# Rope's cosine product on VectorE from PSUM, its sum and a subtraction on GpSimd

## The chip, the cores and the metric

The kernel runs on one core of a Trainium2 chip. A core has five engines with a queue each: TensorE (PE in the profile; its weight loads are PEld), VectorE (DVE), ScalarE (ACT), GpSimd (POOL) and SyncE (SP), which here only issues transfers. Each engine works through its queue in order; an instruction that waits holds up everything behind it on that engine. The metric is the device time of one execution in microseconds, the median of several.

## The reference

One decoder layer on 512 tokens of width 1024, in float32, with two token mixers side by side and an MLP:

```python
h = rms_norm(x, norm_mix)
u, q, kc, vc, ksl, vsl, kwn, vwn, g_nsa, g_merge = split(h @ w_in)
y_pool = pool_mixer(u, ...)                    # causal means over 2, 4, 8, 16 tokens
y_nsa  = nsa_mixer(q, kc, vc, ksl, vsl, kwn, vwn, g_nsa, ...)
merged = sigmoid(g_a) * (y_pool @ w_proj_pool) + sigmoid(g_b) * (y_nsa @ w_proj_nsa)
x = x + merged @ w_out
x = x + square(relu(rms_norm(x, norm_mlp) @ w_ff1)) @ w_ff2
return rms_norm(x, norm_final)
```

The attention mixer has 16 heads of 64 in two groups. Each head has three branches: compressed keys (31 per group), selected blocks, and a window; with 512 tokens the last two are plain causal attention on keys of their own. Queries and keys are rotated first:

```python
def apply_rope(x, cos, sin):
    x1, x2 = split(x, 2, axis=-1)
    rot = concatenate([-x2, x1], axis=-1)
    return x * cos + rot * sin
```

Each softmax subtracts a row's extreme before the exponential. For the compressed branch that is a separate step, and the change touches it.

## The kernel before, in words

Matrix products run in a split form: each float32 operand becomes a high part and a low part (ScalarE copies the high part, VectorE or GpSimd subtracts it from the original for the low part), and three of the four partial products are summed. The weights are loaded in pieces of 512 KB by SyncE and split shortly before use (L345 and L347).

**Stages.** Up to about 30 us the input is normed and transposed. Up to about 175 us the projections run (function `fm`, matmuls at L388), among them the two key projections and the first three query pairs, each followed by a rope. Then comes attention, to about 395 us, and after it the output projections and the MLP.

**Attention.** Work is cut into 96 slots, twelve for each of eight pairs of heads. For slot i the loop at L1096 issues the scores of slot i+1 on TensorE (L977), the transposes of slot i-4's probabilities (L1039, into `psT`) and their evacuation (L1050 on ScalarE, L1054 on VectorE), the masking and row minimum of slot i on VectorE (L999), its exponential on ScalarE (L1009), and the weighting of slot i-1's probabilities on GpSimd (L1022, which needs the reciprocal of L1019 on VectorE). The product with the values (L1073) follows two slots after the transposes. In between, TensorE runs pieces of the remaining projections (the filler: five query pairs and the merge gate).

**Side work.** Generators in the list `side` advance by one step, to their next `yield`, once in each slot (`step_side`, L1121). Two kinds matter here. `rope` (L575) turns one projection of 128 rows and 512 tokens: ScalarE copies it from PSUM to `xr` with a scale, four transfers copy 32-row blocks of `xr` crosswise into `sw`, then come two products with the cosine table in halves of 256 columns (L589, in place in `xr`), two with the sine table (L592, in `sw`), and two sums (L597). Products run on GpSimd when `mode["pool"]` is set, which it is from attention on (five ropes), and on VectorE before (five ropes); the sums run on VectorE always. Then `done` splits the result into high and low part: for queries ScalarE copies at L622 and L623, and VectorE subtracts at L625 and L627. `cmp_scores` (L909) makes the compressed branch's probabilities of one pair: matmuls (L914), mask (L921, L922) and row minimum (L924) on VectorE, the subtraction of the minimum (L926), the exponential on ScalarE (L929), sum and reciprocal on VectorE (L931 to L934), scaling and split on GpSimd (L936 to L939), then transposes (L947) and a copy on ScalarE (L949). There are eight of these.

**What sets the order.** The code above gives program order. The framework's planner then orders each engine's queue: among the instructions that it takes to be ready it prefers the one that is earliest in the program. Operations that the program issues in different slots can so stand next to each other in a queue. `tc.issue_after` pins an instruction behind another one; GpSimd also issues transfers (L267) that add pairs of weight blocks for the MLP, in some slots behind the weighting.

Of the kernel before, what the change touches and what calls it, by code (L numbers as in the profile page):

```python
# [13 lines left out]
F32 = mybir.dt.float32  # L14
FR = mybir.dt.float32r
AF = mybir.ActivationFunctionType
ALU = mybir.AluOpType
# [3 lines left out]
S = 512  # L21
# [41 lines left out]
def trunk(ctx: ExitStack, tc: tile.TileContext, A, out):  # L63
    nc = tc.nc
    PE, ACT, DVE, POOL = nc.tensor, nc.scalar, nc.vector, nc.gpsimd
    PSUM = bass.MemoryType.PSUM

    def pool(name, **kw):
        return tc.tile_pool(name=name, bufs=1, reuse_waits="tile", **kw)
# [400 lines left out]
    op = e2.enter_context(pool("op"))  # L470
# [3 lines left out]
    ap = at.enter_context(pool("att"))  # L474
# [91 lines left out]
    cosT, sinT = cst[:, C_COS:C_COS + S], cst[:, C_SIN:C_SIN + S]  # L566
# [8 lines left out]
    def rope(ps, scale, done, after=0):  # L575

        assert not scored["rope"]
        scored["rope"] = 1
        xr = ap.tile([128, S], F32, tag="rx", bufs=1, name="rx")
        sw = ap.tile([128, S], F32, tag="rs", bufs=1, name="rs")  # L580
        ACT.activation(xr, ps, AF.Copy, scale=scale)
        for b in range(4):
            a = b ^ 1
            nc.sync.dma_start(sw[32 * b:32 * b + 32, :], xr[32 * a:32 * a + 32, :])
        yield
        eng = POOL if mode["pool"] else DVE
        hs = [slice(0, S // 2), slice(S // 2, S)]
        for c in hs:
            eng.tensor_tensor(xr[:, c], xr[:, c], cosT[:, c], op=ALU.mult)  # L589
            yield  # L590
        for c in hs:
            eng.tensor_tensor(sw[:, c], sw[:, c], sinT[:, c], op=ALU.mult)  # L592
            yield
        yield
        for c in hs:
            yield
            DVE.tensor_tensor(xr[:, c], xr[:, c], sw[:, c], op=ALU.add)  # L597
        while scored["pairs"] < after:
            yield
        for _ in done(xr):  # L600
            yield
        scored["rope"] = 0
# [28 lines left out]
    with ExitStack() as c1:  # L631
# [170 lines left out]
        def pool_out(g):  # L802
# [5 lines left out]
                                     op1=ALU.subtract)  # L808

        first_posts += [cmp_first("k"), lambda ps: rope(ps, -0.125, k_done(0))]  # L810
        next(first)
        pr = ps1.tile([128, 36], F32, tag="F", bufs=2, name="psF")
# [4 lines left out]
        for k in P1[2:]:  # L817
            i = int(k[-1]) if k[-1].isdigit() else None
            if k == "kw":
                run(fm(k, ps1, lambda ps: rope(ps, -0.125, k_done(1))))  # L820
            elif k == "cv":
                run(fm(k, ps1, cmp_first("v")))
            elif k[0] == "w" and k != "wpool":
                run(cmp_mlp1(k[1], i))
            elif k[0] == "u":
                run(fm(k, ps1, pool_mix(i)))
            elif k[0] == "q":
                run(fm(k, ps1, lambda ps, i=i: rope(ps, 1.0, q_done(i))))
            elif k == "V0":
                run(project_v())  # L830
            elif k == "wpool":
                use(k)
            elif k[:2] == "ga":
                def post(ps, j=i):
                    ACT.activation(MA[:, j, :], ps, AF.Sigmoid)  # L835
                run(fm(k, ps1, post))
                if i < 4:
                    pool_out(i)
            elif k[:2] == "pp":
                w = use(k)  # L840
                for e in range(2):
                    def post(ps, jj=2 * i + e):
                        DVE.tensor_tensor(MA[:, jj, :], ps, MA[:, jj, :], op=ALU.mult)
                    run(fm(w, ps1, post, xT=yd, sub=e, nk=4))
# [9 lines left out]
    with ExitStack() as c2:  # L854
# [54 lines left out]
        def cmp_scores(p):  # L909
            g = p // 4  # L910
            ps = ps2.tile([128, NT, 2, 64], F32, tag="S", bufs=S_BANKS, name="psC")
            for qb in range(NT):
                for h in range(2):
                    PE.matmul(ps[:, qb, h, :], Q[p][:, h, 128 * qb:128 * qb + 128], KC[g], start=True, stop=True,  # L914
                              skip_group_check=True)
            w = p2.tile([128, NT, 2, 64], F32, tag="cw", bufs=1, name="cw")
            s8 = p2.tile([128, 3, 8], F32, tag="c8", bufs=1, name="c8")
            cm = cst[:, C_CM:C_CM + 128].rearrange("p (q n) -> p q n", q=NT)
            wl = w[:, :, :, 0:32]
            wf = w.rearrange("p q h n -> p (q h) n")[:, :, 0:32]  # L920
            DVE.tensor_tensor(wl, ps[:, :, :, 0:32], cm[:, :, None, :].to_broadcast([128, NT, 2, 32]), op=ALU.add)  # L921
            DVE.tensor_tensor(wl, ps[:, :, :, 32:64], wl, op=ALU.add)  # L922
            yield
            DVE.tensor_reduce(s8[:, 0, :], wf, axis=AX.X, op=ALU.min)  # L924
            yield
            DVE.tensor_tensor(wf, wf, s8[:, 0, :, None].to_broadcast([128, 8, 32]), op=ALU.subtract)  # L926
            yield
            yield
            ACT.activation(wl, wl, AF.Exp, scale=-1.0)  # L929
            yield  # L930
            DVE.tensor_reduce(s8[:, 1, :], wf, axis=AX.X, op=ALU.add)  # L931
            DVE.reciprocal(s8[:, 2, :], s8[:, 1, :])
            r = s8[:, 2, :].rearrange("p (q h) -> p q h", q=NT)
            DVE.tensor_tensor(r, r, GT[:, :, 6 * p:6 * p + 6:3], op=ALU.mult)  # L934
            yield
            POOL.tensor_tensor(wl, wl, r[:, :, :, None].to_broadcast([128, NT, 2, 32]), op=ALU.mult)  # L936
            pH, pL = (PC[:, :, e, :].rearrange("p q (h n) -> p q h n", h=2) for e in range(2))
            POOL.tensor_scalar(pH, wl, 1.0, 1.0, op0=ALU.mult, op1=ALU.mult)
            POOL.tensor_tensor(pL, wl, pH.bitcast(F32), op=ALU.subtract)  # L939
            yield  # L940
            yield
            yield
            yield
            pt = ps2.tile([128, S], F32, tag="T", bufs=T_BANKS, name="psT")
            for qb in range(NT):
                src = PC[:, qb, :, :].rearrange("p e c -> p (e c)")
                PE.transpose(pt[:, 128 * qb:128 * qb + 128].bitcast(FR), src, identR)  # L947
            t = p2.tile([128, S], FR, tag="pc", bufs=1, name="pc")
            ACT.activation(t, pt, AF.Copy)  # L949
            PTc[p] = t  # L950
# [126 lines left out]
        def o_evac(p, half):  # L1077
# [7 lines left out]
            split_ready()  # L1085

        side.append(cmp_scores(0))
        while 0 not in PTc:
            fill()
# [6 lines left out]
        for i in range(n + LAG + PLAG):  # L1096
            if i < n:
                p = slots[i][0]
                if i % 12 == 3 and p + 1 < NPAIR:
                    while p + 1 not in Q:  # L1100
                        fill()
                        step_side()
                if i % 12 == CMP_AT and p + 1 < NPAIR:
                    side.append(cmp_scores(p + 1))
# [476 lines left out]
```

## Time and profile before

| | us |
|---|---|
| median of 3 runs (lowest to highest) | 819.68 (818.72 to 820.07) |
| profiled execution | 819.35 |
| its span, first to last instruction | 817.4 |
| TensorE busy | 791.0 (97%) |
| VectorE busy | 616.8 (75%) |
| ScalarE busy | 483.3 (59%) |
| GpSimd busy | 206.1 (25%) |

A row of the timeline has start, duration, engine, line, operation, the tiles it writes and reads, and the shapes; in brackets stands the idle time of the engine just before it and what ended it. A row of a group has the count, and the duration in ns as lowest, median and highest, or the busy sum and the mean. In a table by stretch, the busy times of PE, PEld, DVE, ACT and POOL follow the stretch's length, each with its number of instructions, then the granted TensorE clock (1.00 is full speed), the busy share of the transfer engines and their GB/s. Rows of GpSimd can overlap, since a following instruction's record begins before the one ahead has ended; the distance between starts tells what one costs in a series.

### The profile page before, as it was taken

To read this page: it belongs to the slowest core of one execution; us is meant where nothing else is said; L and a number is where in the kernel's file an instruction comes from. 1 tells how busy PE (TensorE), PEld (TensorE's weight loads), DVE (VectorE), ACT (ScalarE), POOL (GpSimd) and SP (SyncE) were. 2 spreads that over 40 slices of the span, in tenths; PEclk is the share of its full clock that TensorE was granted. 3 is DMA by queue.
4 is the path that set the end of the run, shared out by engine and by line. 5 is a ranking of instruction groups with operands and counts; after the bars stand their busy time and mean duration, and the time that the engine had idled before them with its cause. 6 is when DMAs were issued, how large, how long until landed. Compare 5 with 4: busy or idle time off the path is not lost.

```text
span 817.4 us, 13940 instructions
## 1 busy us (share of the span) xinstructions
PE 791.0 (97%) x5081; PEld 707.5 (87%) x5081; DVE 616.8 (75%) x1201; ACT 483.3 (59%) x959; POOL 206.1 (25%) x271
## 2 busy tenths in 40 slices
PE   7999999998899999999999999999999999999996
PEld 5889877886788888888787899999999999999985
DVE  7797734548979898889675479996889688987823
ACT  5566433326877888899434466844674377347711
POOL 6000000027757867765333200111010100000000
PEclk9999999999999999999999999999999999999999
DMA  9363732456537634552964716999998965345402
GB/s 304 96 176 107 203 79 92 113 155 154 78 103 136 145 83 91 104 126 56 331 159 135 206 21 186 321 241 287 252 271 228 272 185 181 123 162 180 155 1 103
DMA packets 124445, 130.85 MB, mean 160 GB/s; under 512 B 5173, under 2 KB 112217, under 8 KB 124250
## 3 DMA queue, kind: packets, MB, share of 16 engines
q1 hardware_dynamic: 105082, 110.31, 42.0%
q0 software_dynamic: 19008, 18.88, 16.2%
q8 instruction: 40, 0.66, 0.3%
q10 hardware_dynamic: 288, 0.79, 0.3%
q14 instruction: 27, 0.22, 0.1%
HBM read 125.24 MB, written 39.85 MB: 202 GB/s over the span
## 4 chain that ended last, share of the span: by engine, by line
PE 70%; DVE 16%; ACT 6%; issue 4%; DMA 2%; POOL 1%; SPq 0%; ACTq 0%; DVEq 0%; POOLq 0%
PE psF L388 21%; PE psB L1350 16%; PE psB L388 13%; PE psB L1466 7%; PE psO L1073 3%; PE psT L1039 2%; PE psS L977 2%; DVE wl L302 2%; PE psV L388 2%; DVE P L999 2%; DVE PT L1054 1%; DMA raw<-w_out 1%; ACT P L1009 1%; PE psF L442 1%; DVE w3l L302 1%
## 5 line engine op out<-in xcount | busy, mean ns | idle before, releaser
L388 PE MATMUL psF<-R,wh 128*128 128x512 f32 x512 | 166.9, 404 | 0.2 <-ACT MA L835 0.2
L300 ACT ACTIVATE wh<-raw 128x1024 fp32r<-128x1024 f32 x66 | 69.8, 1058 | 75.6 <-PE psB L1466 33.4
L345 ACT ACTIVATE wh<-raw 128x512 fp32r<-128x512 f32 (+1 forms) x102 | 61.3, 619 | 86.7 <-PE psF L388 35.8
L388 PEld LDWEIGHTS psF<-R,wh 128*128 128x128 f32 x512 | 92.5, 189 | 17.9 <-ACT MA L835 0.5
L388 PE MATMUL psF<-R,wl 128*128 128x512 f32 x256 | 101.9, 398 | 0.8 <-DVE wl L347 0.8
L1022 POOL TENSOR_SCALAR P<-P,sm,GT 128x128 f32<-128x128 f32 (+3 forms) x128 | 85.2, 698 | 47.9 <-DVE sm L1019 33.5
L302 DVE TENSOR_TENSOR wl<-raw,wh 128x1024 fp32r<-128x1024 f32 x66 | 80.7, 1222 | 17.6 <-ACT wh L300 17.5
L267 POOL DMA_DIRECT2D S<-w_ff x36 | 41.7, 1158 | 193.0 <-DMA S<-w_ff 146.3
L347 DVE TENSOR_TENSOR wl<-raw,wh 128x512 fp32r<-128x512 f32 (+1 forms) x78 | 56.2, 732 | 37.7 <-ACT wh L345 37.4
L1009 ACT ACTIVATE P<-P,sm 128x128 f32<-128x128 f32 (+3 forms) x128 | 71.1, 557 | 11.6 <-DVE sm L999 10.5
L1350 PE MATMUL psB<-R,wh 128*128 128x256 f32 x352 | 64.1, 282 | 0.0
L999 DVE CUSTOM_DVE_ANT_0 P<-psS,cst 128x128 f32<-128x128 f32 (+3 forms) x128 | 59.6, 484 | 5.9 <-PE psT L1039 4.3
L347 POOL TENSOR_TENSOR wl<-raw,wh 128x512 fp32r<-128x512 f32 x28 | 39.9, 1427 | 85.1 <-ACT wh L345 82.7
L1054 DVE TENSOR_TENSOR PT<-psT,PT 128x512 fp32r<-128x512 f32 (+2 forms) x96 | 56.7, 595 | 4.6 <-ACT PT L1050 3.6
L1050 ACT ACTIVATE PT<-psT 128x512 fp32r<-128x512 f32 (+2 forms) x96 | 49.3, 521 | 16.0 <-PE psT L1039 15.4
L388 PEld LDWEIGHTS psF<-R,wl 128*128 128x128 f32 x256 | 48.4, 189 | 11.8 <-DVE wl L347 0.9
L1039 PE MATMUL psT<-ident,P 128*128 128x128 f32 x320 | 51.3, 275 | 6.1 <-POOL P L1022 4.9
L300 ACT ACTIVATE w3h<-raw 128x1024 fp32r<-128x1024 f32 x32 | 33.8, 1057 | 38.8 <-PE psB L1466 16.5
L1039 PEld LDWEIGHTS psT<-ident,P 128*128 128x128 f32 x320 | 40.0, 141 | 17.0 <-POOL P L1022 7.8
L1350 PEld LDWEIGHTS psB<-R,wh 128*128 128x128 f32 x352 | 54.1, 189 | 0.3 <-DVE R L1292 0.2
L1350 PE MATMUL psB<-R,wl 128*128 128x256 f32 x176 | 49.5, 281 | 0.0
L302 DVE TENSOR_TENSOR w3l<-raw,w3h 128x1024 fp32r<-128x1024 f32 x32 | 39.1, 1222 | 12.9 <-ACT w3h L300 12.9
(432 smaller groups left out, 2280.3 us busy)
## 6 DMA issues: line engine op xcount, KB each, us to landing
raw<-w_ff SPq DMA_DIRECT2D x56, 512.0 KB, 4.6
S<-w_ff POOLq DMA_DIRECT2D x36, 512.0 KB, 7.6
raw<-S SPq DMA_DIRECT2D x36, 512.0 KB, 5.4
raw<-w_in SPq DMA_DIRECT2D x32, 512.0 KB, 3.9
S<-w_ff SPq DMA_DIRECT2D x28, 512.0 KB, 5.4
S<-S SPq DMA_DIRECT2D x8, 512.0 KB, 8.3
raw<-w_proj_nsa SPq DMA_DIRECT2D x8, 512.0 KB, 4.0
raw<-w_out SPq DMA_DIRECT2D x8, 512.0 KB, 4.4
```

The source lines that it names most:

```text
L300: ACT.activation(h, t, AF.Copy)
L302: DVE.tensor_tensor(l, t, h.bitcast(F32), op=ALU.subtract)
L345: ACT.activation(h[:, sl], t[:, sl], AF.Copy)
L347: eng.tensor_tensor(l[:, sl], t[:, sl], h[:, sl].bitcast(F32), op=ALU.subtract)
L388: PE.matmul(ps, a, b, start=first and j == 0, stop=last and j == n - 1, skip_group_check=True)
L999: DVE.tensor_tensor_reduce(out=P[:, o:o + n].rearrange("p (a c) -> p a c", c=128), in0=s, in1=m, scale=1.0, scalar=3e38, op0=ALU.add, op1= ...
L1009: last_exp[:] = [ACT.activation(c, c, AF.Exp, bias=sm[:, 0, e:e + 1], scale=-1.0, accum_out=sm[:, 1, e:e + 1])]
L1022: r = POOL.tensor_scalar(P[:, o:o + n], P[:, o:o + n], sm[:, 2, e:e + 1], GT[:, qb, c + e:c + e + 1], op0=ALU.mult, op1=ALU.mult)
L1039: PE.transpose(pt[:, 128 * j:128 * j + 128], P[:, 128 * j:128 * j + 128], ident)
L1054: DVE.tensor_tensor(dL, src, dH.bitcast(F32), op=ALU.subtract)
L1350: PE.matmul(out, w[u][:, k, 128 * f:128 * f + 128], XB[x][v][:, k, :], **kw)
L1466: PE.matmul(out, YB[y][u][:, k, 128 * f:128 * f + 128], w[v][:, k, :], **kw)
```

## The change

In `rope` a third tile `xc` takes the cosine product, which VectorE now makes in one instruction from PSUM with the scale in it, in the step that makes ScalarE's copy. The two steps of the old cosine products stay as empty ones, so that the sine products and the sums keep their steps. The sums go to the engine that makes the sine products, GpSimd during attention, and read `xc` in place of `xr`; they still write `xr`. In `cmp_scores` the subtraction of the minimum goes from VectorE to GpSimd.

```diff
         xr = ap.tile([128, S], F32, tag="rx", bufs=1, name="rx")
         sw = ap.tile([128, S], F32, tag="rs", bufs=1, name="rs")
+        xc = ap.tile([128, S], F32, tag="rc", bufs=1, name="rc")
         ACT.activation(xr, ps, AF.Copy, scale=scale)
         for b in range(4):
             a = b ^ 1
             nc.sync.dma_start(sw[32 * b:32 * b + 32, :], xr[32 * a:32 * a + 32, :])
+        DVE.scalar_tensor_tensor(xc, ps, scale, cosT, op0=ALU.mult, op1=ALU.mult)
         yield
         eng = POOL if mode["pool"] else DVE
         hs = [slice(0, S // 2), slice(S // 2, S)]
-        for c in hs:
-            eng.tensor_tensor(xr[:, c], xr[:, c], cosT[:, c], op=ALU.mult)
-            yield
+        yield
+        yield
         for c in hs:
             eng.tensor_tensor(sw[:, c], sw[:, c], sinT[:, c], op=ALU.mult)
             yield
         yield
         for c in hs:
             yield
-            DVE.tensor_tensor(xr[:, c], xr[:, c], sw[:, c], op=ALU.add)
+            eng.tensor_tensor(xr[:, c], xc[:, c], sw[:, c], op=ALU.add)
...
-            DVE.tensor_tensor(wf, wf, s8[:, 0, :, None].to_broadcast([128, 8, 32]), op=ALU.subtract)
+            POOL.tensor_tensor(wf, wf, s8[:, 0, :, None].to_broadcast([128, 8, 32]), op=ALU.subtract)
```

## The prediction

> **What bounds the kernel now.** I read the page first, then busy time by stretch, then TensorE's waits, and last the timelines of the two places that these point to.
>
> ```profile
> span 817.4 us, 13940 instructions
> PE 791.0 (97%) x5081; PEld 707.5 (87%) x5081; DVE 616.8 (75%) x1201; ACT 483.3 (59%) x959; POOL 206.1 (25%) x271
> ```
> ```profile
> 30.00:175.00 145.00, 144.80 (x701) 120.34 (x700) 92.75 (x182) 67.46 (x128) 2.41 (x6) 1.00 0.47 132
> 175.00:230.00 55.00, 49.01 (x280) 41.03 (x279) 44.11 (x135) 36.80 (x99) 36.75 (x53) 0.94 0.51 106
> 230.00:380.00 150.00, 147.34 (x943) 128.98 (x942) 131.40 (x435) 125.42 (x339) 104.96 (x146) 1.00 0.51 111
> 380.00:817.00 437.00, 425.63 (x3028) 397.34 (x3026) 328.69 (x421) 236.31 (x363) 48.91 (x40) 1.00 0.66 188
> ```
>
> After each stretch's length stand the busy times of PE, PEld, DVE, ACT and POOL, then the granted clock. TensorE bounds the kernel: from 30 to 175 us, where the first five ropes run, it idles 0.2 us. The stretch to look at is 175 to 230, the start of attention: 6.0 us idle (55.00 less 49.01) and a clock of 0.94. From 230 to 380 it idles 2.7 us. TensorE's waits in these two stretches (total us, times, longest):
>
> ```profile
> PE psT L1039 <- POOL P L1022: 4.9, 3, 2.4
> ...
> PE psF L388 <- DVE wl L347: 0.8, 1, 0.8
> PE psO L1064 <- DVE oT L1082: 0.8, 3, 0.3
> PE psT L1039 <- ACT pc L949: 0.7, 1, 0.7
> PE psT L947 <- DVE sm L1019: 0.3, 1, 0.3
> ```
>
> The first line is of 175 to 230: the transposes wait for GpSimd's weighting of the probabilities, three times. The other four are all there is from 230 to 380, and none waits for GpSimd. The three waits in TensorE's timeline, with another one far from here for comparison:
>
> ```profile
> 193.62 0.39 PE L388 MATMUL psF<-R,wl 128*128 128x512 f32 x1
> 196.17 0.44 PE L1039 MATMUL psT<-ident,P 128*128 128x128 f32 x2 [2.16 <-POOL P L1022]
> 196.94 0.44 PE L1039 MATMUL psT<-ident,P 128*128 128x128 f32 x2 [0.33 <-POOL P L1022]
> ...
> 217.90 0.34 PE L977 MATMUL psS<-KL,Q 128*128 128x384 f32 x1
> 220.68 0.44 PE L1039 MATMUL psT<-ident,P 128*128 128x128 f32 x2 [2.44 <-POOL P L1022]
> ...
> 398.51 0.70 PE L388 MATMUL psB<-R,wh 128*128 128x512 f32 x2 [1.67 <-ACT mH L1250]
> ```
> ```profile
> 197.86:201.28 3.42, 3.07 (x10) 2.10 (x10) 2.88 (x11) 2.08 (x7) 2.30 (x3) 0.50 0.42 153
> ...
> 221.76:225.17 3.41, 3.41 (x14) 3.04 (x13) 3.16 (x10) 2.03 (x5) 2.16 (x5) 0.50 0.00 0
> ...
> 396.00:402.00 6.00, 4.33 (x19) 3.25 (x18) 5.88 (x7) 2.42 (x4) 2.79 (x2) 1.00 1.13 306
> ```
>
> Each long stall is followed by about 3.4 us at half clock, which costs 3.41 x 0.5 = 1.7 us; the 1.67 us stall at 396.8 kept full clock. So a stall of 2.2 to 2.4 us costs about 4 us, and one under 1.7 us only itself.
>
> Why GpSimd was late, in its timeline at both places:
>
> ```profile
> 190.49 1.09 POOL L1022 TENSOR_SCALAR P<-P,sm,GT 128x256 f32<-128x256 f32 x2
> ...
> 192.41 1.83 POOL L589 TENSOR_TENSOR rx<-rx,cst 128x256 f32<-128x256 f32 x2
> 193.81 1.78 POOL L592 TENSOR_TENSOR rs<-rs,cst 128x256 f32<-128x256 f32 x2
> 195.20 2.31 POOL L1022 TENSOR_SCALAR P<-P,sm,GT 128x256 f32<-128x256 f32 x3
> ...
> 217.31 1.86 POOL L589 TENSOR_TENSOR rx<-rx,cst 128x256 f32<-128x256 f32 x2
> 218.68 1.17 POOL L592 TENSOR_TENSOR rs<-rs,cst 128x256 f32<-128x256 f32 x1
> 219.39 1.76 POOL L1022 TENSOR_SCALAR P<-P,sm,GT 128x256 f32<-128x256 f32 x2
> ```
> ```profile
> 192.42 4.15 DVE L926 TENSOR_TENSOR cw<-cw,c 128x256 f32<-128x256 f32 x1
> ...
> 197.10 1.03 DVE L597 TENSOR_TENSOR rx<-rx,rs 128x256 f32<-128x256 f32 x2
> ...
> 217.44 2.79 DVE L926 TENSOR_TENSOR cw<-cw,c 128x256 f32<-128x256 f32 x1
> ```
>
> Rope products stand in GpSimd's queue ahead of the weighting that TensorE waits for: four at 192.41, three at 217.31, each (195.20 - 192.41) / 4 = 0.70 us by the distance of their starts. At the same two moments VectorE sits 4.15 and 2.79 us in one subtraction whose shortest run is 0.41 us (next rows). So one series of GpSimd products, with operands from SBUF, delays TensorE through GpSimd's queue and holds VectorE, which asks for two operands from SBUF itself.
>
> **The change part by part.**
>
> ```profile
> L926 DVE TENSOR_TENSOR cw<-cw,c x8: 412/556/4149, 177.0 to 346.1; 128x256 f32<-128x256 f32 x8
> ...
> L597 DVE TENSOR_TENSOR rx<-rx,rs x20: 397/420/1710, 41.5 to 321.6; 128x256 f32<-128x256 f32 x20
> ...
> L589 POOL TENSOR_TENSOR rx<-rx,cst x10: 727/741/1190, 192.4 to 318.9; 128x256 f32<-128x256 f32 x10
> ...
> L936 POOL TENSOR_TENSOR cw<-cw,c x8: 609/616/617, 180.2 to 353.8; 128x256 f32<-128x256 f32 x8
> ...
> L807 DVE SCALAR_TENSOR_TENSOR yd<-psF,pec,yd x4: 750/752/752, 97.5 to 123.8; 128x512 fp32r<-128x512 f32 x4
> ```
>
> *First five ropes (VectorE does all).* Two products go, 0.42 each like the sums of L597 (same shape, same engine); one of 512 columns from PSUM comes, 0.75 by L807, the nearest row. The new product also holds the PSUM bank until VectorE has read it, where ScalarE's copy alone did. VectorE is busy 92.75 of 145 us there and TensorE idles 0.2: 0 us. Without that cover the cost is 5 x (0.75 - 0.84), a small gain, up to five late banks at 0.75 each, 3.8 us.
>
> *Last five ropes, VectorE.* Two sums go, one product from PSUM comes. At the first place that is 1.03 us (197.10) against 0.75. The PSUM product is issued beside ScalarE's copy, before the swap transfers, and so before GpSimd's series begins. Held like the subtraction it could lose 4.15 - 0.42 = 3.7 us; running clear it loses 0. I take 0, since nothing of the series stands beside it. The Trainium skill (SBUF, Who interferes with whom) says that a VectorE instruction with two SBUF inputs contends with a GpSimd instruction reading SBUF, one with a single such input not: the rule would give 0 in any position, and the subtraction's 4.15 us agree with its first half. The copies to the swapped halves stay, four transfers on the same queue, behind the same ScalarE copy.
>
> *Last five ropes, GpSimd.* Two cosine products go, two sums come, of one shape and so at 0.70 each. The sum of work stays; its place moves. The cosine pair waited for the swap copies and came with the sine pair in one block; each sum is issued four slots after its sine product, with weightings ahead of it in the program. So the block ahead of the weighting is halved.
>
> *The subtraction.* Off VectorE go 4.15, 2.79 and six short ones; onto GpSimd come eight of 0.62 (L936: same shape, same broadcast). The planner may place it ahead of a weighting, +0.62, or behind it, 0. ScalarE's exponential (L929) now waits for GpSimd, with the slots' exponentials and evacuations queued behind it.
>
> *First stall.* The weighting starts after two products, 192.41 + 1.40 = 193.81, and takes (by half of 1.09 for a pair unhindered at the shape's 0.55) to 194.36; TensorE runs dry at 193.62 + 0.39 = 194.01. Idle 0.4 instead of 2.16, the 0.33 shrinks to 0.1: 2.0 saved, and 1.7 of half clock. If the subtraction goes ahead, 0.6 less. VectorE, whose freed 3.7 us feed the next weightings, no longer holds them back.
>
> *Second stall.* Sine product at 217.31, weighting at 218.01, done at 218.56; TensorE dry at 217.90 + 0.34 = 218.24. Idle 0.3 instead of 2.44: 2.1, plus 1.7; with the subtraction ahead 3.2 in all.
>
> The trace can't say which place it gets, so I take it behind at the first and ahead at the second: 3.7 + 3.2 = 6.9 us. Bounds: 0 (both stalls stay over 1.7) to 7.5.
>
> *From 230 on.* TensorE waits for no GpSimd result there, so the five subtractions left cost 0 us, ScalarE's wait for them included; without that cover it is 5 x 0.62 = 3.1. VectorE's relief could return up to the 1.9 us of waits for it (0.8 + 0.8 + 0.3). One spot speaks against: the fourth of these ropes.
>
> ```profile
> 287.23 1.14 POOL L1022 TENSOR_SCALAR P<-P,sm,GT 128x512 f32<-128x512 f32 x1
> 289.81 2.16 POOL L1022 TENSOR_SCALAR P<-P,sm,GT 128x128 f32<-128x128 f32 x4 [1.44 <-DVE sm L1019]
> ...
> 289.54 0.40 DVE L597 TENSOR_TENSOR rx<-rx,rs 128x256 f32<-128x256 f32 x1
> ...
> 289.97 0.64 ACT L622 ACTIVATE Q<-rx 64x512 fp32r<-64x512 f32 x1
> ...
> 291.67 0.59 ACT L949 ACTIVATE pc<-psT 128x512 fp32r<-128x512 f32 x1
> ```
>
> ScalarE copies q right after the last sum (289.54 + 0.40 to 289.97), and behind that in its queue stands the copy that TensorE waits 0.7 us for. On GpSimd the sum fits the idle 1.44 us, 0 lost, or lands behind the four weightings, 289.81 + 2.16 + 0.70 = 292.67, 2.7 us later. I take a quarter: -0.7.
>
> Sum: 819.35 (the profiled run, 817.4 of span) less 6.9 plus 0.7 = 813.15. The median, 819.68, lies 0.33 above the profiled run, so the forecast is 813.5. From 398 on TensorE is dense and simply starts 6 us sooner.
>
> **The rivals.**
>
> *One stall stays.* If at one place the weighting still ends 1.7 us after TensorE ran dry, its half clock stays too: 819.68 - 3.7 + 0.7 = 816.7. For it: the planner placed a weighting behind every ready rope product so far.
>
> *Nothing moves.* VectorE's remaining two-operand SBUF work (L347, L625, L627) gets held instead, by the sums: 819.7, give or take 1.6. Against it: the long holds in the rows above, 4.15, 2.79 and at most 1.71, are the subtraction's and the sum's, and both leave VectorE.
>
> *GpSimd's queue is the bound (slower).* Before 230 the weightings have no slack, as TensorE's three waits show. If sums and subtraction are placed ahead of it as well, the first stall's block is two sine products, a subtraction and two sums, 1.40 + 0.62 + 1.40 = 3.42 against 2.79, and the second's likewise: +0.6 each, both half clocks stay, and the later ScalarE hand-over costs up to 2.7: 819.68 + 1.2 + 2.7 = 823.6. It decides from the point where more than 2.8 us stand ahead of a weighting. For it: GpSimd is already busy 36.75 of 55 us there. Against it: the sums' program place is behind those weightings.
>
> The Trainium skill (GPSIMD Engine Reference, 4.1 Engine selection) speaks against the change: two-input elementwise work belongs on VectorE, GpSimd being about 2x slower. Here 0.70 stands against 0.42, 1.7x; charged to the path, 10 x 0.28 + 8 x 0.20 = 4.4 us, that rule would give 824.1.
>
> **How the numbers follow.** Forecast (811 to 816) 0.55; one stall stays (816 to 818) 0.15; nothing moves 0.09; slower 0.21. A measurement tells about 0.2%, 1.6 us: faster is the first two, 0.70; same 0.09; slower 0.21. The range leaves out the best case, both stalls gone and VectorE's 1.9 us returned (0.06), and the worse half of the slow one: 810.5 to 822. The forecast's own is 811 to 816.
>
> **What would show it.** Right: in 175 to 230 TensorE idle near 2 us and clock 1.00; no VectorE instruction over 1.5 us; sine products followed by a weighting, not by sums. Wrong: a clock of 0.50 anywhere from 190 to 230, TensorE waiting for L1022 after 230, or ScalarE's L622 waiting for GpSimd over 1 us. The planner orders all queues anew from the changed program, and a new order far from the ropes would make me wrong with every step above right.

## The result and the profile after

| | us |
|---|---|
| before, median of 9 runs | 819.83 (818.72 to 820.86) |
| after, median of 9 runs | 822.13 (821.18 to 824.65) |
| after by before | 1.0032, 95% interval 1.0022 to 1.0043 |
| profiled execution of after, and its span | 822.13, 820.2 |

The change makes the kernel 0.32% slower; forecast were 813.5 us, 0.8% faster. Line numbers of after are one higher from L582 on: the weighting is L1023, the evacuations L1051 (ScalarE) and L1055 (VectorE), the sums L598, the subtraction L927, its exponential L930, query's copies L623 and L624.

The table by stretch of after, in the columns of the prediction:

```profile
30.00:175.00 145.00, 144.80 (x702) 120.34 (x700) 92.27 (x178) 67.94 (x129) 1.73 (x6) 1.00 0.48 132
175.00:230.00 55.00, 50.66 (x304) 42.20 (x304) 40.18 (x141) 39.41 (x107) 40.31 (x59) 1.00 0.52 106
230.00:380.00 150.00, 142.53 (x900) 122.75 (x899) 122.66 (x409) 118.75 (x325) 102.25 (x145) 1.00 0.51 110
```

Two things happened. From 175 to 230 the clock is 1.00 instead of 0.94 and TensorE idles 4.3 us instead of 6.0: the gain is there. From 230 to 380 it idles 7.5 us instead of 2.7: there it is lost again. Compared by the starts of the same transposes in the two traces, after leads by 4.3 us at 221 us (time of before) and 4.4 at 239, by 3.8 at 248, 2.0 at 260 and 0.0 at 272; it lags by 2.4 at 289, 2.5 at 356, and 3.1 at 767 (the points at 239 and 767 by the starts of L388's matmuls).

TensorE's waits of after, from 175 to 230 (total us, times, longest):

```profile
PE psT L1040 <- POOL P L1023: 1.9, 2, 1.5
PE psO L1074 <- ACT PT L1051: 1.5, 1, 1.5
```

and from 230 to 380:

```profile
PE psT L1040 <- DVE PT L1055: 2.9, 3, 1.8
PE psO L1065 <- DVE oT L1083: 2.0, 2, 1.0
PE psT L948 <- DVE PT L1055: 1.6, 2, 1.1
PE psF L388 <- DVE wl L347: 0.8, 1, 0.8
```

TensorE still waits for no GpSimd result after 230. It waits for VectorE's evacuations, and these for ScalarE. ScalarE's waits of after from 175 to 380:

```profile
ACT cw L930 <- POOL cw L927: 12.7, 7, 4.4
...
ACT Q L623 <- POOL rx L598: 3.2, 2, 1.7
```

ScalarE stands 12.7 us in front of seven of the eight exponentials of the compressed scores, until GpSimd has subtracted, and 3.2 us in front of two of the query copies, until GpSimd has summed. Up to 230 us this is no loss: 5.0 of the 12.7 us lie there, and in the kernel before ScalarE waited 7.9 us there for the subtraction on VectorE (the second line is of a wait at 177 us, with the loading of a table behind it):

```profile
ACT cw L929 <- DVE cw L926: 4.7, 2, 3.3
...
ACT L929 <- DVE cw L926: 3.2, 1, 3.2
```

From 230 to 380 the kernel before has no such wait in its list, and after has 7.7 us of it in four waits. The longest, in the timelines of GpSimd, ScalarE, VectorE and TensorE of after:

```profile
241.31 1.90 POOL L593 TENSOR_TENSOR rs<-rs,cst 128x256 f32<-128x256 f32 x2
242.71 1.76 POOL L347 TENSOR_TENSOR wl<-raw,wh 128x512 fp32r<-128x512 f32 x1
243.97 1.87 POOL L598 TENSOR_TENSOR rx<-rc,rs 128x256 f32<-128x256 f32 x2
245.39 2.13 POOL L1023 TENSOR_SCALAR P<-P,sm,GT 128x256 f32<-128x256 f32 x3
247.10 0.99 POOL L927 TENSOR_TENSOR cw<-cw,c 128x256 f32<-128x256 f32 x1
```
```profile
248.12 0.42 ACT L930 ACTIVATE cw<-cw 128x256 f32<-128x256 f32 x1 [4.39 <-POOL cw L927]
248.44 0.37 ACT L1051 ACTIVATE PT<-psT 128x256 fp32r<-128x256 f32 x1
```
```profile
244.37 0.42 DVE L925 TENSOR_REDUCE c<-cw 128x8 f32<-128x256 f32 x1
...
248.57 0.42 DVE L932 TENSOR_REDUCE c<-cw 128x8 f32<-128x256 f32 x1 [2.84 <-ACT cw L930]
248.91 0.41 DVE L1055 TENSOR_TENSOR PT<-psT,PT 128x256 fp32r<-128x256 f32 x1
```
```profile
249.46 0.63 PE L1040 MATMUL psT<-ident,P 128*128 128x128 f32 x4 [0.84 <-DVE PT L1055]
```

The row minimum is ready at 244.37 + 0.42 = 244.79. The subtraction could start then, but GpSimd has only just begun the second of two sums, three weightings follow ahead of it in the queue, and it starts at 247.10. ScalarE, in order, waits 4.39 us; behind it stands the evacuation L1051; VectorE idles 2.84 us; TensorE runs dry for 0.84 us. A subtraction of 0.4 us has become a hand-over from VectorE to GpSimd to ScalarE and back.

The places where the stalls of before were look like this in after, on GpSimd and on TensorE:

```profile
192.59 1.77 POOL L593 TENSOR_TENSOR rs<-rs,cst 128x256 f32<-128x256 f32 x2
193.99 1.05 POOL L598 TENSOR_TENSOR rx<-rc,rs 128x256 f32<-128x256 f32 x1
194.70 1.38 POOL L1023 TENSOR_SCALAR P<-P,sm,GT 128x256 f32<-128x256 f32 x2
...
216.41 1.18 POOL L593 TENSOR_TENSOR rs<-rs,cst 128x256 f32<-128x256 f32 x1
217.11 1.05 POOL L927 TENSOR_TENSOR cw<-cw,c 128x256 f32<-128x256 f32 x1
217.68 1.84 POOL L598 TENSOR_TENSOR rx<-rc,rs 128x256 f32<-128x256 f32 x2
219.09 1.06 POOL L1023 TENSOR_SCALAR P<-P,sm,GT 128x384 f32<-128x384 f32 x1
```
```profile
195.61 0.96 PE L1040 MATMUL psT<-ident,P 128*128 128x128 f32 x4 [1.50 <-POOL P L1023]
...
197.45 0.55 PE L1040 MATMUL psT<-ident,P 128*128 128x128 f32 x3 [0.42 <-POOL P L1023]
...
220.37 0.39 PE L1074 MATMUL psO<-PT,VV 128*128 128x256 f32 x1 [1.46 <-ACT PT L1051]
```

The sums do go ahead of the weightings: one at the first place, two with the subtraction at the second. The stalls shrink from 2.16 to 1.50 and from 2.44 to 1.46 us, and no half clock follows either. The second one has changed its cause: it is ScalarE's evacuation now, which stood behind the exponential that waited 2.17 us for the subtraction of 217.11:

```profile
218.19 0.42 ACT L930 ACTIVATE cw<-cw 128x256 f32<-128x256 f32 x1 [2.17 <-POOL cw L927]
...
219.23 1.08 ACT L1051 ACTIVATE PT<-psT 128x512 fp32r<-128x512 f32 x2
```

### The profile page after: what moved, and what is told of

Same layout as the page of the kernel before. It is cut to its first block, busy times and chain, and to the rows that moved or that the text cites. A ratio compares the mean times of both kernels' runs of the same rounds, so it can differ in the third digit from the quotient of the medians.

```text
span 820.2 us, 13927 instructions
## 1 busy us (share of the span) xinstructions
PE 790.5 (96%) x5081; PEld 704.8 (86%) x5081; DVE 606.3 (74%) x1183; ACT 482.4 (59%) x959; POOL 207.9 (25%) x279
## 4 chain that ended last, share of the span: by engine, by line
PE 64%; DVE 16%; ACT 7%; issue 5%; POOL 4%; DMA 3%; ACTq 0%; POOLq 0%; DVEq 0%; SPq 0%
PE psF L388 20%; PE psB L1351 13%; PE psB L388 12%; PE psB L1467 7%; DVE wl L302 2%; PE psO L1074 2%; PE psT L1040 2%; PE psS L978 2%; PE psV L388 2%; POOL P L1023 2%; DMA raw<-w_out 1%; ACT P L1010 1%; DVE P L1000 1%; DVE w3l L302 1%; PE psF L442 1%
## 5 line engine op out<-in xcount | busy, mean ns | idle before, releaser
L388 PE MATMUL psF<-R,wh 128*128 128x512 f32 x512 | 166.6, 403 | 0.2 <-ACT MA L836 0.2
L388 PEld LDWEIGHTS psF<-R,wh 128*128 128x128 f32 x512 | 92.2, 188 | 17.9 <-ACT MA L836 0.5
L388 PE MATMUL psF<-R,wl 128*128 128x512 f32 x256 | 101.4, 396 | 0.8 <-DVE wl L347 0.8
L1023 POOL TENSOR_SCALAR P<-P,sm,GT 128x128 f32<-128x128 f32 (+3 forms) x128 | 85.6, 702 | 48.4 <-DVE sm L1020 34.7
L347 DVE TENSOR_TENSOR wl<-raw,wh 128x512 fp32r<-128x512 f32 (+1 forms) x78 | 57.0, 742 | 39.6 <-ACT wh L345 38.4
L347 POOL TENSOR_TENSOR wl<-raw,wh 128x512 fp32r<-128x512 f32 x28 | 39.6, 1418 | 87.6 <-ACT wh L345 85.3
L1055 DVE TENSOR_TENSOR PT<-psT,PT 128x512 fp32r<-128x512 f32 (+2 forms) x96 | 56.5, 594 | 7.2 <-ACT PT L1051 6.4
L388 PEld LDWEIGHTS psF<-R,wl 128*128 128x128 f32 x256 | 48.1, 188 | 12.3 <-DVE wl L347 1.3
L1051 ACT ACTIVATE PT<-psT 128x512 fp32r<-128x512 f32 (+2 forms) x96 | 48.9, 519 | 12.3 <-PE psT L1040 11.6
L1074 PE MATMUL psO<-PT,VV 128*128 128x256 f32 x320 | 48.0, 285 | 1.5 <-ACT PT L1051 1.5
```

The lines of the kernel that those rows point to most:

```text
L347: eng.tensor_tensor(l[:, sl], t[:, sl], h[:, sl].bitcast(F32), op=ALU.subtract)
L388: PE.matmul(ps, a, b, start=first and j == 0, stop=last and j == n - 1, skip_group_check=True)
L1023: r = POOL.tensor_scalar(P[:, o:o + n], P[:, o:o + n], sm[:, 2, e:e + 1], GT[:, qb, c + e:c + e + 1], op0=ALU.mult, op1=ALU.mult)
L1074: PE.matmul(ps[:, qb % 2, :, :], VV[:, k, b, g, :], t[:, j, :, :], start=False, stop=last and j == len(kbs) - 1 and t is tL, skip_group_ch ...
```

## The experiments

Three theories were set against each other: that what costs is VectorE being **held** beside GpSimd's series (H); that it is **ScalarE's wait** for results moved to GpSimd (W); and that it is the **amount of work** on VectorE (V). Some expectations name further rivals of their own; the first four name the planner's new order (P). Times of before on the chips of the three batches: 820.62, 820.31 and 820.34 us. All ratios are to the before of the same batch, with their 95% intervals, and where kernels of two batches are compared, each is taken as its difference from its own before (after: +2.3 us).

**The parts alone.** The cosine product from PSUM alone, with sums and subtraction on VectorE:

```diff
-            eng.tensor_tensor(xr[:, c], xc[:, c], sw[:, c], op=ALU.add)
+            DVE.tensor_tensor(xr[:, c], xc[:, c], sw[:, c], op=ALU.add)
...
-            POOL.tensor_tensor(wf, wf, s8[:, 0, :, None].to_broadcast([128, 8, 32]), op=ALU.subtract)
+            DVE.tensor_tensor(wf, wf, s8[:, 0, :, None].to_broadcast([128, 8, 32]), op=ALU.subtract)
```

> The cosine product alone on VectorE from PSUM; sums and subtraction stay on VectorE. Theory W: GpSimd's series is halved, neither ScalarE instruction waits for GpSimd, the subtraction on VectorE may still be held beside the two sine products (under 2 us in place of 4.15): TensorE gains 3 to 4 us by 240 us and keeps them, 815 to 817. Theory P: no relation to the parts.

Measured: 817.64 us (816.08 to 820.43), ratio 0.9963 (0.9948 to 0.9978). The product alone is a gain of 3.0 us, the time just above theory W's range. Product and subtraction on GpSimd, sums on VectorE (the first of the two edits above):

> Cosine product on VectorE from PSUM and the subtraction on GpSimd; the sums stay on VectorE. Theory W: the early gain of about 4 us, the loss of about 4 us between 244 and 268 behind the subtraction, but not the 1.8 us at 289: 818.5 to 820.5. Theory P: no relation to the parts.

Measured: 821.33 us (819.39 to 823.2), ratio 1.0008 (0.9994 to 1.0022): the subtraction costs 3.7 us on top of the product, and the time is just above theory W's range. Product and sums, subtraction on VectorE (the second edit above):

> The rope part of the change alone: cosine product on VectorE from PSUM, sums on GpSimd; the compressed scores' subtraction stays on VectorE. Theory W (the loss is ScalarE waiting for GpSimd: 12.7 us of its exponential behind the moved subtraction, 3.2 us of the query copies behind the moved sums): the exponential's wait for GpSimd goes, the copies' wait of 3.2 us and the 1.8 us stall of TensorE at 289 stay, so 817 to 820. Theory P (the planner's new order costs the time, whatever was moved): no relation to the parts, 821 or more is as likely as 818.

Measured: 826.33 us (825.4 to 827.77), ratio 1.0065 (1.0045 to 1.0085): 5.7 us slower than before, far above theory W's range, no surprise to theory P, and slower than the full change. The group of the subtraction in this kernel, and its worst one in VectorE's and GpSimd's timelines:

```profile
L927 DVE TENSOR_TENSOR cw<-cw,c x8: 415/501/4578, 177.7 to 353.0; 128x256 f32<-128x256 f32 x8
```
```profile
193.61 4.58 DVE L927 TENSOR_TENSOR cw<-cw,c 128x256 f32<-128x256 f32 x1
198.11 0.68 DVE L1000 CUSTOM_DVE_ANT_0 P<-psS,cst 128x512 f32<-128x512 f32 x1
```
```profile
193.11 1.78 POOL L593 TENSOR_TENSOR rs<-rs,cst 128x256 f32<-128x256 f32 x2
194.50 1.06 POOL L598 TENSOR_TENSOR rx<-rc,rs 128x256 f32<-128x256 f32 x1
195.21 1.39 POOL L1023 TENSOR_SCALAR P<-P,sm,GT 128x256 f32<-128x256 f32 x2
196.27 1.02 POOL L598 TENSOR_TENSOR rx<-rc,rs 128x256 f32<-128x256 f32 x1
196.98 0.93 POOL L1023 TENSOR_SCALAR P<-P,sm,GT 128x384 f32<-128x384 f32 x1
```

The subtraction begins inside a series of seven GpSimd instructions and ends at 198.19 (193.61 + 4.58), when that series is over (196.98 + 0.93 = 197.91). VectorE's next masking starts some 4 us late. So with the sums on GpSimd, a subtraction left on VectorE is held still longer than in the kernel before. That is why moving both costs less than moving the sums alone.

The subtraction alone, rope as before:

```diff
-            DVE.tensor_tensor(wf, wf, s8[:, 0, :, None].to_broadcast([128, 8, 32]), op=ALU.subtract)
+            POOL.tensor_tensor(wf, wf, s8[:, 0, :, None].to_broadcast([128, 8, 32]), op=ALU.subtract)
```

> The subtraction alone on GpSimd; rope as before. Theory W: GpSimd's series of four products stays ahead of the weighting, so both half-clock stretches stay or nearly so, and ScalarE waits over 8 us for the subtraction: 821 to 824. Theory P: no relation to the parts.

Measured: 826.10 us (824.5 to 827.01), ratio 1.0059 (1.0039 to 1.0079), above the range. The hold passes on to the next VectorE instruction with two operands in SBUF, here the sums, of which three take 3.0 to 3.2 us; in the group of the sums:

```profile
L597 DVE TENSOR_TENSOR rx<-rx,rs x20: 399/418/3170, 41.9 to 327.2; 128x256 f32<-128x256 f32 x20
```

**The hold by itself.** As the product and sums alone, but the masked scores stay in PSUM, so that minimum and subtraction on VectorE read them there and the subtraction has one operand from SBUF (the lines that name the parts of the score tile and the minimum's own are left out; the subtraction is L929 here):

```diff
-            DVE.tensor_tensor(wl, ps[:, :, :, 32:64], wl, op=ALU.add)
+            DVE.tensor_tensor(pm, ps[:, :, :, 32:64], wl, op=ALU.add)
...
-            DVE.tensor_tensor(wf, wf, s8[:, 0, :, None].to_broadcast([128, 8, 32]), op=ALU.subtract)
+            DVE.tensor_tensor(wf, pf, s8[:, 0, :, None].to_broadcast([128, 8, 32]), op=ALU.subtract)
```

> The rope part alone (826.3 when the subtraction stays on VectorE with both operands in SBUF), but the masked scores are kept in PSUM, so that the subtraction on VectorE has one operand in PSUM and one in SBUF. Theory H: its 4.6 us at two places fall below 1.0, both half-clock stretches go or shrink, 819 to 822.5. Theory Q (GpSimd's queue ahead of the weighting is what costs, not the hold): 825 or more, the subtraction's duration aside.

Measured: 817.18 us (815.61 to 819.59), ratio 0.9966 (0.9953 to 0.9979), better than expected. The group of the subtraction:

```profile
L929 DVE TENSOR_TENSOR cw<-psC,c x8: 403/415/424, 176.5 to 342.0; 128x256 f32<-128x256 f32 x8
```

Same shape, same engine, and GpSimd has the same sine products, sums and weightings to do, in the same order at both places; what differs is where the masked scores lie. Twice the subtraction stands beside sine products (at 192.45 and 214.99) and takes 0.42 and 0.41 us. 4.58 us become 0.42 at most, and the time, each against its own before, falls by 8.8 us (from +5.7 to -3.1). This shows the hold, and the price of all that follows from it; theory P, by which it doesn't matter what was moved, doesn't explain it. By the profiled executions 5.1 us of the price are the clock: the kernel with the subtraction held runs 10.24 us at half clock between 200 and 231 us, and this one none there. The same edit on the product alone (sums on VectorE):

> The cosine product alone (817.6), with the masked scores kept in PSUM as well. Theory H: only one hold of the subtraction is left there to take away (2.0 us), so 816 to 818; the PSUM bank is held two steps longer, which may give up to 1 us back.

Measured: 816.44 us (814.46 to 818.0), ratio 0.995 (0.9937 to 0.9963), as expected.

**Nothing of rope on GpSimd.** Product from PSUM, sine products, sums and subtraction all on VectorE:

```diff
-        eng = POOL if mode["pool"] else DVE
+        eng = DVE
```

(with the two edits of the product alone)

> The cosine product on VectorE from PSUM, and the sine products, the sums and the subtraction on VectorE too, in all ten ropes; GpSimd has no rope work. Theory H (VectorE's instructions with two SBUF operands wait out GpSimd's series, and the series stands ahead of the weighting): no series is left, the subtraction runs in 0.4 to 1.0 us, TensorE's 1.4 us of waits for the weighting before 230 go, and the time falls below the 817.6 of the cosine alone: 815.5 to 817. Theory V (VectorE's amount of work counts): ten more products of 0.42 on VectorE during attention give up to 4 us back, 818 to 822.

Measured: 814.64 us (813.39 to 814.99), ratio 0.9933 (0.992 to 0.9946): better than theory H expected, 5.7 us faster than before and 8.0 below after, though VectorE has more to do (1211 instructions on this kernel's page, 1201 on that of before, 1183 on that of after). The amount of work on VectorE is not what bounds. Its table by stretch and the group of its subtraction:

```profile
175.00:230.00 55.00, 54.72 (x330) 45.62 (x329) 45.51 (x156) 42.32 (x114) 35.43 (x50) 1.00 0.52 106
230.00:380.00 150.00, 146.32 (x929) 127.97 (x928) 133.51 (x439) 125.01 (x334) 96.79 (x132) 0.99 0.51 111
```
```profile
L927 DVE TENSOR_TENSOR cw<-cw,c x8: 406/416/632, 177.1 to 340.5; 128x256 f32<-128x256 f32 x8
```

TensorE idles 0.3 us from 175 to 230. The clock of 0.99 is one stretch of 3.41 us at half clock, from 232.69. The same with the masked scores in PSUM as well:

> Whole rope on VectorE with the cosine product from PSUM, and the masked compressed scores kept in PSUM so that the subtraction on VectorE has one operand from SBUF. With GpSimd's rope series gone there is nothing left that held the subtraction (0.41 to 0.63 us in the kernel with the rope on VectorE), so theory H expects the same as that kernel, 813.5 to 815.5. [...]

Measured: 814.78 us (814.17 to 815.06), ratio 0.9925 (0.9909 to 0.9941), as expected. With no series left to be held by, the operand's place makes no difference. And the kernel before with that one line, `eng = DVE`, and no product from PSUM:

> The kernel before with one edit: all ten ropes run on VectorE as they stand, cosine products from SBUF, no product from PSUM; GpSimd has no rope work. Theory C (what pays is that GpSimd's series is gone from beside VectorE and from ahead of the weighting): 813.5 to 816.5, subtraction under 0.7 us each, TensorE idle in 175 to 230 under 1 us. Rival P (the product from PSUM is needed for the gain, since it takes some of VectorE's work away: five times 0.16 us by the rows, and an earlier end of each rope): 817 to 819.5.

Measured: 817.68 us (815.43 to 820.9), ratio 0.9967 (0.9951 to 0.9983). This is rival P's range: by the median the product from PSUM is needed for half of the gain, and the interval just misses that of the kernel with the product (0.992 to 0.9946). What the product does for it isn't shown, since the range of this kernel is wide, and its profiled execution is the fastest (815.43). In that execution TensorE has one stall as long as those of before.

**ScalarE's wait.** To let the exponential come later, two more steps were put ahead of it in the full change:

```diff
+            yield
+            yield
             ACT.activation(wl, wl, AF.Exp, scale=-1.0)
```

> The full change, with the compressed branch's exponential two steps (slots) later in the program. Theory W (ScalarE stands behind the subtraction on GpSimd for 12.7 us in all, and that is what loses the lead of 4.4 us after 240): ScalarE's wait for the subtraction falls below 5 us, the stalls of TensorE at 249, 260 and 265 shrink, 818.5 to 821. If the wait is not the cause: 822 as the full change.

Measured: 825.87 us (825.27 to 826.51), ratio 1.007 (1.0058 to 1.0082). It didn't do what it was made for: ScalarE's wait for the subtraction is still 11.0 us, the longest 3.7, and the order of the queues changed elsewhere, with stalls of TensorE at other places (1.83 us at 196.9, 1.36 at 234.9) and a stretch at half clock from 213.99 to 217.40 that after doesn't have. It says nothing on the theory; it says that two steps in a side generator can cost 3.3 us, 1.7 of them by the clock.

So the subtraction was put back instead, from the fourth pair on (after 230 us), with the operand in PSUM so that it isn't held; the first three stay on GpSimd (the subtraction is L930 here, its exponential L933, VectorE's evacuation L1058):

```diff
+            late = p >= 3
...
-            POOL.tensor_tensor(wf, wf, s8[:, 0, :, None].to_broadcast([128, 8, 32]), op=ALU.subtract)
+            (DVE if late else POOL).tensor_tensor(wf, pf if late else wf, s8[:, 0, :, None].to_broadcast([128, 8, 32]), op=ALU.subtract)
```

> The full change, but from the fourth pair on (after 230 us) the subtraction is on VectorE with its first operand kept in PSUM; the first three stay on GpSimd. Theory W (after 230 us the 4.4 us lead is lost because ScalarE waits for the subtraction on GpSimd): ScalarE's wait for L927 falls under 2 us after 230, the lead at 272 us is still over 3 us, and the time is 816 to 819. Rival S (it is lost to the sums on GpSimd and to VectorE's two-operand work beside them, L347 and L626, and the planner's new order): lead at 272 under 1.5 us, time 820 to 823.

Measured: 820.05 us (818.6 to 821.98), ratio 0.9994 (0.9983 to 1.0004), at the lower edge of rival S's range, and the lead at 272 is 2.2 us, between what the two theories expected. ScalarE's wait for the subtraction from 230 to 380:

```profile
ACT cw L933 <- DVE cw L930: 0.6, 1, 0.6
```

The 7.7 us that ScalarE waited for the subtraction after 230 in the full change (four times) are 0.6 here, and TensorE stands 2.2 us better at 272, the median 2.6 us better (-0.3 against +2.3). Between 221 and 272 after loses the whole of its lead of 4.3 us, and this kernel 1.5 us (3.7 to 2.2). So the five subtractions cost 2.7 of the 4.3. The 1.5 us stay in this kernel, and the largest piece is another hold. VectorE's and GpSimd's timelines of it:

```profile
260.62 1.81 DVE L626 TENSOR_TENSOR Q<-rx,Q 64x512 fp32r<-64x512 f32 x1
...
262.97 0.54 DVE L1058 TENSOR_TENSOR PT<-psT,PT 128x384 fp32r<-128x384 f32 x1
```
```profile
260.61 1.28 POOL L347 TENSOR_TENSOR wl<-raw,wh 128x512 fp32r<-128x512 f32 x1 [2.26 <-ACT wh L345]
```

The low part of the query, 0.69 us at its shortest, and the low part of a weight block on GpSimd start in the same moment, the first takes 1.81 us, and the evacuation behind it makes TensorE wait 1.05 us. In after the same pair meets at 262.8 (1.83 us, TensorE's wait 1.15). In the kernel before, where it is L625, it takes 1.02 us at most, as its group shows:

```profile
L625 DVE TENSOR_TENSOR Q<-rx,Q x8: 684/770/1022, 99.9 to 324.8; 64x512 fp32r<-64x512 f32 x8
```

At last the subtraction on GpSimd without any rope there:

```diff
-        eng = POOL if mode["pool"] else DVE
+        eng = DVE
```

(with the sums on VectorE, the subtraction on GpSimd as in after)

> The whole rope is on VectorE and GpSimd has no rope work; only the subtraction of the minimum is on GpSimd. Compared with the kernel that has the whole rope on VectorE and the subtraction there too (814.64 us). Theory W (ScalarE's wait for a subtraction on GpSimd costs by itself, because evacuations stand behind the exponential): ScalarE's total wait for L927 stays over 8 us and the time is 817 to 820. Rival R (the wait is long only because rope instructions stand ahead of the subtraction in GpSimd's queue): ScalarE's longest wait for it falls under 2 us and the time is 814 to 816.

Measured: 815.56 us (814.16 to 816.7), ratio 0.9933 (0.9917 to 0.995). ScalarE's wait for the subtraction from 175 to 380:

```profile
ACT cw L930 <- POOL cw L927: 5.7, 5, 2.0
```

It is 5.7 us instead of 12.7, the longest 2.0 instead of 4.4, and the time is in rival R's range. Against the kernel with the subtraction on VectorE it costs 0.9 us by the medians and nothing by the ratios (0.9933 both), so no cost is shown. The subtraction on GpSimd is cheap as long as GpSimd's queue has no rope series ahead of it: less than 1 us without rope there, 3.7 us with the sine products alone.

## Why the prediction was wrong

In the profiled executions 6.2 us were to be gained and 2.8 us were lost (822.13 against 819.35), 9.0 us apart. By the leads above, 2.6 of them are missing at the two stalls, 4.3 went between 221 and 272 where nothing was forecast, 1.6 more than forecast went at the fourth rope's sums, and about 0.5 elsewhere.

*From 230 on: the five subtractions at 0 us, ScalarE's wait included.* This is the step that failed. It was argued from TensorE's waits, that none is for GpSimd. That remained true, and didn't help: the wait went through ScalarE's queue, evacuation, VectorE, TensorE. Putting these five back returned 2.6 us in the median, and 2.7 of the 4.3 us in the trace. The price "without that cover", 3.1, was near it by luck: it sums durations on GpSimd, and the loss is a wait for what stood ahead of the subtraction. The other 1.5 us, mostly the hold of the query's low part, are in no term of the sum. The rows for a better reading were there: TensorE's waits of before from 230 to 380 are all for VectorE and ScalarE, so what delays either of these two has no cover, whoever delays it.

*The fourth rope's sums, -0.7.* Mechanism right, size not. ScalarE's copy waits 1.67 us for GpSimd's sum (at 287.67), the query's second copy and then an evacuation stand behind it, and TensorE waits 1.84 us at 291.25. Between 283 and 289 the two traces part by 2.3 us, inside the bounds 0 to 2.7, and near their upper end rather than at a quarter.

*First and second stall, -6.9.* The mechanism was right: both half clocks are gone, and the subtraction no longer holds VectorE there. The size was not: idle 1.50 and 1.46 instead of 0.4 and 0.3, and a lead of 4.3 us. The step that failed is "each sum is issued four slots after its sine product, with weightings ahead of it in the program", from which followed that the sums stay behind. The planner put one sum ahead of the first weighting (193.99) and two sums with the subtraction ahead of the second (217.11 to 219.09). At the second place TensorE no longer waited for the weighting, but for the evacuation behind ScalarE's exponential. No half clock followed them, as forecast; the 1.84 us stall at 291.25 kept full clock too, so a stall over 1.7 us needn't cost a half clock (see the last section).

*Product from PSUM, 0 us; first five ropes, 0 us.* All ten products take 680 to 693 ns, though four of the five in attention run while GpSimd works; none is held, and TensorE idles 0.2 us from 30 to 175 as before. That agrees with the rule quoted from the Trainium skill (SBUF — State Buffer, Who interferes with whom), by which one SBUF input doesn't contend. Alone this part gives 3.0 us, which the prediction had shared out over the stalls: it halves the block ahead of the weighting, with nothing moved onto GpSimd.

*The rivals.* "Nothing moves" had its mechanism come true at one place: the query's low part was held, 1.83 us, though by L347 rather than by the sums. The slower rival's time, 823.6, was near the result partly by luck: its hand-over on ScalarE came about, but the half clocks it counted on didn't, both went. The rule of the Trainium skill's GPSIMD Engine Reference (4.1 Engine selection), two-input work belongs on VectorE, had the sign right, and the kernel with all of rope there is the fastest one. Its 824.1, the difference of durations charged to the path, isn't what the traces show: the sums alone cost 8.7 us over the product alone (826.33 against 817.64), of which ten times 0.28 would be 2.8.

*Of the signs given ahead:* right were the clock of 1.00, and no wait of TensorE for the weighting after 230. Wrong were idle near 2 (4.3), no VectorE instruction over 1.5 us (1.83), a weighting right behind the sine products (a sum at 193.99), and ScalarE's query copy waiting over 1 us for GpSimd (1.67).

What stays open is the rest after 289: the two traces part by another 0.1 us up to 356 and 0.5 us in the MLP, where the program is the same and only the order can differ. No run isolates that.

## What to carry to other kernels

Before an instruction is moved to an engine with room, follow its result to whoever reads it, and look at what stands behind the reader in its queue: engine time can be free while the hand-over isn't. A wait list that doesn't name an engine shows that its results are in time now, not that results moved to it will be. Where VectorE and GpSimd work side by side, one operand read from PSUM was worth more than moving the work (8.8 us against 3.4 for the subtraction, with the sums on GpSimd), and here it was best to keep the rope's two-operand work all on one engine.

## What the runs showed of the hardware

A VectorE instruction with two operands in SBUF was held through several GpSimd instructions and not just through one of them: twice 4.58 us beside seven (with the product and the sums moved), where it takes 0.42 us with one operand in PSUM. Both of these holds ended only after the seven. That isn't always so: in the kernel before the subtraction ended at 196.57, while GpSimd's weightings ran on to 197.51.

A stall's length alone doesn't say whether the clock halves. In the kernel before 2.16 us was followed by 3.4 us at half clock; in the kernel with the plain rope on VectorE 2.14 us wasn't; and in the kernel with all of rope and the product from PSUM on VectorE two stalls of 0.78 and 1.01 us were. The 2.14 us in TensorE's timeline:

```profile
327.14 0.63 PE L1039 MATMUL psT<-ident,P 128*128 128x128 f32 x4 [2.14 <-DVE sm L1019]
```

The half-clock stretches begin and end in step: in all traces each one between 30 and 800 us lasts 3.41 us or twice that, and the two of the kernel before begin 23.90 us apart, seven times 3.41. Cut into steps of that length which end where such a stretch begins (for the kernel with the plain rope it is the one at the run's idle end, from 811.23), the first two lines below are of the kernel with all of rope on VectorE, the last two of the one with the plain rope:

```profile
229.28:232.69 3.41, 1.62 (x10) 1.19 (x10) 3.35 (x4) 1.50 (x5) 2.39 (x2) 1.00 0.00 0
232.69:236.10 3.41, 3.41 (x10) 2.63 (x9) 2.61 (x14) 1.97 (x8) 1.67 (x4) 0.50 0.79 205
...
323.12:326.53 3.41, 1.88 (x14) 1.44 (x12) 3.41 (x4) 3.36 (x9) 3.41 (x5) 1.00 0.76 93
326.53:329.95 3.42, 2.72 (x17) 2.28 (x17) 3.33 (x10) 1.70 (x5) 2.70 (x4) 1.00 0.96 227
```

The two short stalls fall into one step, with 1.79 of 3.41 us idle, and the 2.14 us are split between two, with 1.53 and 0.70 us idle in all. Of all the steps at full clock between 30 and 800 us, in thirteen of the fourteen traces, half clock follows each of the seven with 1.71 us idle or more (half of a step), and none with 1.69 or less. The fourteenth, the kernel with the later exponential, breaks this both ways: 1.83 us idle in a step were followed by full clock, 0.96 us by half. So idle time within a step fits far better than a stall's length, and isn't shown to be the whole rule.

The eleven executions of the kernel with the plain rope range from 815.43 to 820.9 us, and the mean granted clock of the same executions from 0.999 down to 0.993. That fits stalls at the edge, which cost their half clock in some executions and not in others; only one of them has a trace, so this is argued, not shown.
